# Turning the last pair's values one step later, and re-spacing the splits, row turns and early products of steps 46 to 63

## The chip, the cores and the metric

The kernel runs on one core of one Trainium2 chip. Its time is the device time of one execution in microseconds (us). Before the change the median of three runs is 1219.77 us (1219.66 to 1220.37).

The core has five engines that run side by side, each through its own list of instructions in order: TensorE (PE, matrix products and transposes), VectorE (DVE), ScalarE (ACT), GpSimd (POOL) and SyncE (SP), which here issues all DMA transfers. An instruction that needs another engine's result waits for it, and everything behind it on its own engine waits too.

## What is computed

One decoder layer on 1024 tokens of width 1024, in float32. Two mixers read one projection of the normalised input: an attention of eight heads with three dilated windows, and a gated linear recurrence (HGRN) of four heads. Their outputs, one beside the other, go through an output projection, then comes a feed-forward part.

```python
p = rmsnorm(x, mix_pre_norm) @ w_in            # q, k, v of attention; q, f, i, g of HGRN
A = dilated_mixture_attention(q_a, k_a, v_a)   # (window, dilation) = (128,1), (512,4), (2048,16)
R = hgrn2_recurrence(q_h, f_h, i_h, g_h)
x = x + rmsnorm(concat([rmsnorm(A), R]) @ w_out)
x = x + rmsnorm(square(relu(rmsnorm(x) @ w_ff1)) @ w_ff2)
```

## The kernel before

**Products.** Every float32 product is made of three matmuls (`three_pass`, L88 to L91): each factor is split into a high and a low part, and high by high, high by low and low by high are summed in PSUM. A split of a weight piece of 128x1024 is one instruction on ACT (L85, the high part) and one on DVE (L86, the low part); then SP issues the load of a later piece into a freed buffer (L106). `w_get(n, 0)` makes piece n available. The eight pieces of the output projection are WO0 to WO0+7: the first four belong to the HGRN half of its input, the last four to the attention half.

**PSUM.** There are four kinds of banks, two of each, used in turn: "mm" for projections, "s" for the attention's scores (looks), "t" for transposes (turns) and "pv" for weighted values. A bank is taken again once the engines that read it have done so.

**Attention.** The loop of 64 steps (8 heads of 8 items: D0 to D3 and F0, F1, N0, N1, the blocks of the dilated windows) is written out by hand, and the order of the code is the order on each engine. A step's parts are: `raise_` (ACT exponentials, L892), `look` (PE scores L837, L838, then DVE adds the bias table and takes the maximum, L842), `turn` (PE transposes the exponentials, L902, L911 or L914; ACT and DVE write high and low part, L924 to L932), `weigh` (PE multiplies with values, L948, L960, L966) and `finish` (PE transposes the result, L986, DVE sums, L990, POOL scales, L991). The bias table of a head comes from DRAM (`load_bias`, L798); that of the last head, number 7, goes into the tile `etable`.

**Filler.** Between these PE does units of other work, of three matmuls each: up to step 47 projections of later head pairs (`attn_proj`), from then on early products (`early_out`, tiles `pwe`), the HGRN half of the output projection for the first four row tiles, 32 units in all. `UNITS[head][item]` says how many units a step has; half of them, rounded down, stand ahead of the weigh, the rest behind it. An early product needs the row tile turned (`row_turn(t, 0)`, L1078, into `emt`) and the weight pieces; ACT moves its sum out (L1101, `esum`).

**Values of a pair.** The last step of a pair's projection multiplies its value half with a row factor on DVE (L764, tile `vf`, read from PSUM `pm_av`). `values_turn` (L712 to L726) transposes that on PE (L716, tile `pvt`), splits it (ACT L719, DVE L720), and for the second half SP writes the pair's values to DRAM (L723, four transfers `vd`). `far_load` (L642, six transfers, again called `vf`) then reads them back in another order for the far blocks F (L960). Pair 3 holds heads 6 and 7.

**Other pieces around the change.** `row_rec` (POOL, L1035) multiplies a row tile by a gain, `row_load` fetches a finished attention row, `row_norm` sums its squares on ACT (L1044, L1050), `row_gain` scales it on POOL. `hooks[s]` lists what step s does besides its fixed parts, after the first half of its units, the weigh and the finish. After step 63 come the late products (`late_out`, tiles `pwo`), the attention half of the output projection.

Of the kernel before, what the change touches and what calls it, by code (L numbers as in the profile page):

```python
# [25 lines left out]
AH = 8  # L26
# [11 lines left out]
def hymba_layer(ctx, tc, x, w_in, w_out, w_ff1, w_ff2, g_pre, lb_logits, g_mix, g_post,  # L38
# [17 lines left out]
    def bank(tag, name):  # L56
        return ps.tile([P, 512], F32, tag=tag, name=name,
                       bufs={"mm": 2, "s": 2, "t": 2, "pv": 2}[tag])
# [66 lines left out]
    def w_get(i, ahead=1):  # L125
        while done[1] < min(i + 1 + ahead, len(stream)):
            w_split()
        return parts[i]
# [26 lines left out]
    WO0 = len(stream)  # L155
# [13 lines left out]
    queue = []  # L169
# [17 lines left out]
    def drain():  # L187
        while queue:
            n = len(queue)
            fill(1e9)  # L190
            assert len(queue) < n or not queue
# [517 lines left out]
        for t in (kh, kl):  # L709
            nc.sync.dma_start(out=f32(t[c:d]), in_=f32(t[a:b]))  # L710

    def values_turn():  # L712
        pr, vs, full, hf = turn_later.pop(0)
        pt = bank("mm", f"pvt{pr}{hf}")
        for j in range(4):
            TE.transpose(pt[:, j * P:(j + 1) * P], full[:, j * P:(j + 1) * P], ident)  # L716
        ptv = pt.rearrange("p (j h d) -> p j h d", j=4, h=2)
        dst = vs[:, hf * 4:hf * 4 + 4]
        S.activation(dst[:, :, :, 0, :], ptv, AF.Copy)  # L719
        V.tensor_tensor(out=dst[:, :, :, 1, :], in0=ptv, in1=f32(dst[:, :, :, 0, :]), op=ALU.subtract)  # L720
        if hf == 1:
            for r in range(DIL):
                nc.sync.dma_start(out=v_dram[pr][r].rearrange("(n i) c -> i n c", i=32),  # L723
                                  in_=f32(vs[32 * r:32 * r + 32]).rearrange("p n h a d -> p n (h a d)"))
            if pr == 0:
                far_load(0)  # L726
# [68 lines left out]
    def load_bias(hd):  # L795
        if hd < AH and hd not in bts:
            bts[hd] = slab("BT", f"bt{hd}") if hd < AH - 1 else early["table"][:, 0]
            nc.sync.dma_start(out=bts[hd][:, :NEAR + FAR], in_=table_dram[hd])  # L798
# [201 lines left out]
    def load_gain(name, tag, src):  # L1000
        gains[name] = slab(tag, name)
        nc.sync.dma_start(out=gains[name], in_=src.partition_broadcast(P))

    NE = 4
# [14 lines left out]
    def early_sums():  # L1019
        early["sum"] = [wide.tile([P, 2, D], F32, tag="A", name=f"esum{q}") for q in range(NE // 2)]  # L1020
# [4 lines left out]
    def row_load(t):  # L1025
        row = rows[t] = slab("S", f"row{t}")
        c = AW if t < NE else 0
        nc.sync.dma_start(out=row[:, c:AW + AL], in_=mix_dram[t * P:(t + 1) * P, c:AW + AL])
# [4 lines left out]
    def row_rec(t):  # L1033
        gain = gains["early"] if t < NE else gains["gmix"][:, :AW]
        G.tensor_tensor(out=rec_row(t), in0=rec_row(t), in1=gain, op=ALU.mult)  # L1035
# [4 lines left out]
    def row_norm(t, which=(0, 1)):  # L1040
        row = rows[t]
        if 0 in which:
            ss = scales["part", t] = col("ass", 2)
            S.activation(half(f"dm{t}")[:, :AL], row[:, AW:AW + AL], AF.Square, accum_out=ss[:, 0:1])  # L1044
        if 1 not in which:
            return
        ss = scales.pop(("part", t))
        sa = col("asa")
        ra = scales["row", t] = tp.tile([P, 1], F32, tag="era", name=f"era{t}") if t < NE else col("ara")
        S.activation(half(f"dn{t}")[:, AL:AW], row_fin(t), AF.Square, accum_out=ss[:, 1:2])  # L1050
        G.tensor_tensor(out=sa, in0=ss[:, 0:1], in1=ss[:, 1:2], op=ALU.add)
        rsqrt_mean(ra, sa, AW, 1)
# [13 lines left out]
    def row_turn(t, which, late=False, tag="t"):  # L1066

        if t < NE and which == 0:
            dst = early["mt"][t // 2][:, t % 2]
        else:  # L1070
            if (t, 1) not in mts and (t, 0) not in mts or t < NE:
                mts[t] = slab("V8", f"mt{t}", F32R, (P, 2, 2, 4, P))
            dst = mts[t][:, which]
        mts[t, which] = dst
        src = rec_row(t) if which == 0 else rows[t][:, AW:]
        pt = bank("pv" if late else tag, f"pmt{t}_{which}")
        for j in range(4):
            TE.transpose(pt[:, j * P:(j + 1) * P], src[:, j * P:(j + 1) * P], ident)  # L1078
        split_into(dst[:, 0], dst[:, 1], pt.rearrange("p (j c) -> p j c", j=4))
# [12 lines left out]
    def early_out(t):  # L1092
        pms = [bank("mm", f"pwe{t}_{hf}") for hf in range(2)]
        for j in range(4):
            while j >= done[1] - WO0:
                yield None
            for hf, pm in enumerate(pms):
                sl = slice(hf * 512, hf * 512 + 512)
                three_pass(pm, [mts[t, 0][:, i, j] for i in range(2)], [w[:, sl] for w in parts[WO0 + j]], j == 0, j == 3)
                if j == 3:  # L1100
                    S.activation(early_sum(t)[:, sl], pm, AF.Copy)  # L1101
                yield 650.0
# [102 lines left out]
    for h in range(HH):  # L1205
# [5 lines left out]
        if not last:  # L1211
# [1 line left out]

    hooks = {
        0: lambda: last_gate(0),
        1: lambda: last_gate(1),
        43: lambda: row_rec(0),
        44: lambda: [row_rec(1), w_get(WO0, 0)],
        45: lambda: w_get(WO0 + 1, 0),
        46: lambda: [row_turn(0, 0), w_get(WO0 + 2, 0)],  # L1220
        47: lambda: [w_get(WO0 + 3, 0), row_rec(2)],
        49: lambda: [row_turn(1, 0), load_bias(AH - 1), row_rec(3)],
        51: lambda: row_turn(2, 0),
        52: lambda: load_gain("gmix", "R", g_mix),
        55: lambda: [row_load(t) for t in range(2)],
        57: lambda: [row_norm(t, (0,)) for t in range(2)],
        58: lambda: w_get(WO0 + 4, 0),
        59: lambda: [row_norm(0, (1,)), row_gain(0), row_load(2)],
        60: lambda: [row_norm(1, (1,)), row_gain(1)],
        61: lambda: row_turn(0, 1, tag="t"),  # L1230
        62: lambda: w_get(WO0 + 5, 0),
        63: lambda: w_get(WO0 + 6, 0),
    }
    UNITS = ((2, 3, 3, 4, 3, 3, 3, 3), (2, 3, 3, 4, 3, 3, 3, 3), (3, 3, 3, 4, 2, 3, 3, 2), (3, 3, 3, 4, 2, 3, 3, 2),
             (3, 3, 3, 3, 2, 3, 3, 2), (3, 3, 3, 3, 2, 2, 2, 2), (3, 2, 2, 3, 2, 2, 2, 1), (2, 2, 2, 3, 1, 2, 2, 1))
    ITEMS = (("D", 0), ("D", 1), ("D", 2), ("D", 3), ("F", 0), ("F", 1), ("N", 0), ("N", 1))
    LOOKS = {0: ((0, "D", 2), (0, "N", 1)), 1: ((0, "D", 3), (0, "F", 0)), 2: ((0, "F", 1),),
             6: ((1, "D", 0),), 7: ((1, "D", 1),)}
# [3 lines left out]
    for s in range(n_steps):  # L1242
        hd, i = divmod(s, 8)
        if s % 16 == 3:
            first_done[s // 16] = True
        elif s % 16 == 11:
            second_done[s // 16] = True
        ready, to_weigh = to_weigh, []
        if i in (3, 4):
            joint(hd, int(i == 4))  # L1250
        coming = (hd, *ITEMS[i + 1]) if i < 7 else (hd + 1, *ITEMS[0])
        raise_(*coming, which=(0,))
        if s % 16 in (11, 13) and s < n_steps - 16:
            while keys_done[s // 16 + 1] < (1 if s % 16 == 11 else 2):
                fill(1.0)
        looks = LOOKS.get(i, ())
        for d, kind, g in looks[:1]:
            look(hd + d, kind, g)
        kind, g = ITEMS[i]
        turn(hd, kind, g)  # L1260
        raise_(*coming, which=(1,))
        if i == 0:
            far_queries(hd)
        if kind != "D" or g % 2:
            to_weigh.append((hd, kind, g // 2 if kind == "D" else g))
        units = UNITS[hd][i]
        for _ in range(units // 2):
            fill(0.0, True)
        to_fold, last_fold = [(*w, r) for w in ready for r in [weigh(*w)] if r is not None], to_fold
        for d, kind, g in looks[1:]:  # L1270
            look(hd + d, kind, g)
        for *w, r in last_fold:
            finish(*w, *r)
        if i in (0, 2):
            spread_max(hd, int(i == 2))
        elif i == 5:
            send(hd)
        elif i == 6:
            receive(hd)
        if i in (1, 2, 3, 6, 7):  # L1280
            key_job()
        if s == 47:
            drain()
            values_turn()
            early_sums()
            queue.extend(early_out(t) for t in range(NE))
        if s % 16 == 15 and s < n_steps - 1:
            far_load(s // 16 + 1)
        hooks.get(s, lambda: None)()
        for _ in range(units - units // 2):  # L1290
            fill(0.0, True)
        if i in (1, 3):
            swap_max(hd, int(i == 3))
        if i == 7:
            look(hd + 1, "N", 0)
        if s == 53:
            row_turn(3, 0, tag="s")
    for *w, r in to_fold:
        finish(*w, *r)
    drain()  # L1300
# [904 lines left out]
```

## Time and profile before

| | |
|---|---|
| median of three runs | 1219.77 us |
| the profiled execution | 1219.76 us |
| its span, first to last instruction | 1218.0 us |
| PE busy | 1200.7 us, 99% of the span |
| DVE, ACT, POOL busy | 71%, 45%, 27% |
| steps 46 to 63 in the trace | about 462 to 524 us |
| mean granted clock of PE over the span | 0.997 |

In rows of waits the engine and line that waited stand first, then the engine and line that ended the wait, then us in total, times, and the longest. In a timeline a row has start, duration, engine, line, operation, out<-in and shape; a number in brackets at its end is the idle time before it and what ended it. PE matmuls are pipelined: the distance between two starts is what one costs, and its duration is longer. The granted clock is the share of full speed that PE was given.

### The profile page before, as it was taken

Reading aid. Unit: us, or ns where it says so; the run is one execution under the profiler, and the core shown is the slowest. Engines: PE = TensorE matmul, PEld = TensorE weight load, DVE = VectorE, ACT = ScalarE, POOL = GpSimd, SP = SyncE. Lnnn points to the kernel's source line nnn. Section 1 sums busy time; section 2 is a strip of 40 time slices with the busy share of each in tenths; the row PEclk is TensorE's granted clock in tenths of the full one; section 3 lists DMA queues with packets and bytes.
Section 4 is the critical chain, followed back from the end, with each engine's and each line's share of the span. In section 5 each row is a group of like instructions: output and inputs, shape, how many; then the busy total and the mean of one; then the engine's idle time right before and its main releaser. Section 6 shows DMA issues by size and latency. Waiting matters only on the chain.

```text
span 1218.0 us, 17222 instructions
## 1 busy us (share of the span) xinstructions
PE 1200.7 (99%) x6350; PEld 1028.1 (84%) x6350; DVE 868.3 (71%) x1478; ACT 546.9 (45%) x1067; POOL 323.4 (27%) x321
## 2 busy tenths in 40 slices
PE   8999999999999998999999999999999999999998
PEld 8898989888888887878888888888888888888886
DVE  5697878776766767668589567666678454488796
ACT  7633333322665667755565132222234453534562
POOL 0110102022221223245240876665722000000022
PEclk9999999999999999999999999999999999999999
DMA  5221323123443646264425446454587534433337
GB/s 217 68 94 57 113 66 97 47 81 83 133 120 104 156 109 166 77 208 136 172 77 174 172 157 228 178 185 152 190 316 267 216 100 156 156 104 94 115 104 276
DMA packets 86483, 174.21 MB, mean 143 GB/s; under 512 B 12160, under 2 KB 38784, under 8 KB 86400
## 3 DMA queue, kind: packets, MB, share of 16 engines
q1 hardware_dynamic: 86400, 173.12, 43.7%
q8 instruction: 50, 0.82, 0.3%
q14 instruction: 33, 0.27, 0.1%
HBM read 117.76 MB, written 49.04 MB: 137 GB/s over the span
## 4 chain that ended last, share of the span: by engine, by line
PE 94%; ACT 2%; DVE 2%; issue 1%; DMA 1%; SPq 0%; POOL 0%; DVEq 0%; POOLq 0%; ACTq 0%
PE f L1945 18%; PE f2s L1945 7%; PE pig L91 2%; PE pig L89 2%; PE pig L90 2%; PE pl L480 2%; PE pwo L90 2%; PE pwo L91 2%; PE pwo L89 2%; PE pm_f L89 1%; PE pm_ak L89 1%; PE pm_f L91 1%; PE pm_f L90 1%; PE pm_ak L91 1%; PE pm_ak L90 1%; PE pm_av L89 1%
## 5 line engine op out<-in xcount | busy, mean ns | idle before, releaser
L86 DVE TENSOR_TENSOR al<-ar,ah 128x1024 fp32r<-128x1024 f32 x56 | 70.6, 1260 | 80.2 <-ACT ah L85 77.7
L1945 PE MATMUL f<-bh,al 128*128 128x512 f32 x320 | 124.5, 389 | 0.0
L1945 PE MATMUL f<-bh,ah 128*128 128x512 f32 x320 | 124.5, 389 | 0.0
L1945 PE MATMUL f<-bl,ah 128*128 128x512 f32 x320 | 124.5, 389 | 0.0
L85 ACT ACTIVATE ah<-ar 128x1024 fp32r<-128x1024 f32 x56 | 59.1, 1056 | 86.2 <-DMA ar<-actd 85.9
L1945 PEld LDWEIGHTS f<-bh,al 128*128 128x128 f32 x320 | 60.1, 188 | 12.6
L1945 PEld LDWEIGHTS f<-bl,ah 128*128 128x128 f32 x320 | 60.1, 188 | 12.5
L1945 PEld LDWEIGHTS f<-bh,ah 128*128 128x128 f32 x320 | 60.1, 188 | 12.3
L2019 POOL TENSOR_SCALAR lbl<-ssq 128x1 f32<-128x1 f32 x4 | 3.3, 818 | 245.5 <-ACT fd L2015 245.4
L1568 POOL TENSOR_TENSOR e<-x,e 128x512 f32<-128x512 f32 x14 | 21.6, 1540 | 131.3 <-DVE x L1519 131.3
L1945 PE MATMUL f2s<-bh,al 128*128 128x512 f32 (+1 forms) x128 | 49.0, 382 | 0.0
L1945 PE MATMUL f2s<-bl,ah 128*128 128x512 f32 (+1 forms) x128 | 48.9, 382 | 0.0
L1945 PE MATMUL f2s<-bh,ah 128*128 128x512 f32 (+1 forms) x128 | 48.9, 382 | 0.0
L671 POOL COPY tout<-traw 128x256 f32<-128x256 f32 x16 | 12.4, 775 | 109.7 <-DMA traw<-in_bias_tab_dram 76.1
L991 POOL TENSOR_TENSOR anat<-anat,stat 128x128 f32<-128x128 f32 (+1 forms) x24 | 12.4, 515 | 108.2 <-DVE anat L990 91.2
L86 DVE TENSOR_TENSOR bl<-br,bh 128x1024 fp32r<-128x1024 f32 x32 | 40.1, 1252 | 1.2 <-ACT bh L85 1.1
L1962 ACT ACTIVATE acc<-f 128x512 f32<-128x512 f32 x28 | 16.8, 598 | 50.0 <-PE f L1945 50.0
L86 DVE TENSOR_TENSOR wl<-raw,wh 128x1024 fp32r<-128x1024 f32 x23 | 30.6, 1331 | 11.0 <-ACT wh L85 11.0
L85 ACT ACTIVATE bh<-br 128x1024 fp32r<-128x1024 f32 x32 | 33.6, 1051 | 4.2 <-PE f L1945 3.1
L707 POOL TENSOR_TENSOR kl<-kf,kh 64x512 fp32r<-64x512 f32 x16 | 22.2, 1389 | 39.2 <-ACT kh L706 37.1
L751 POOL TENSOR_TENSOR ql<-qf,q 64x512 fp32r<-64x512 f32 x16 | 21.4, 1336 | 42.3 <-ACT q L750 41.7
L89 PE MATMUL pwo<-woh,mt 128*128 128x512 f32 x80 | 31.8, 398 | 0.4 <-ACT woh L85 0.4
(1702 smaller groups left out, 4023.7 us busy)
## 6 DMA issues: line engine op xcount, KB each, us to landing
ar<-actd SPq DMA_DIRECT2D x56, 512.0 KB, 3.7
br<-in_w_ff_dram SPq DMA_DIRECT2D x16, 1024.0 KB, 5.9
w1r<-in_w_ff_dram SPq DMA_DIRECT2D x14, 1024.0 KB, 6.5
raw<-in_w_in_dram SPq DMA_DIRECT2D x26, 512.0 KB, 3.7
actd<-e SPq DMA_DIRECT2D x17, 768.0 KB, 4.3
actd<-e SPq DMA_DIRECT2D x11, 1024.0 KB, 4.1
vd<-v SPq DMA_DIRECT2D x16, 256.0 KB, 4.1
raw<-in_w_out_dram SPq DMA_DIRECT2D x8, 512.0 KB, 3.7
```

The lines of the kernel that those rows point to most:

```text
L85: S.activation(hi, src, AF.Copy)
L86: eng.tensor_tensor(out=lo, in0=src, in1=f32(hi), op=ALU.subtract)
L89: TE.matmul(dst, lhs[0], rhs[0], start=start, stop=False)
L90: TE.matmul(dst, lhs[0], rhs[1], start=False, stop=False)
L91: TE.matmul(dst, lhs[1], rhs[0], start=False, stop=stop)
L480: TE.matmul(pl[:, n % 2, :192], kt[:, n * P:(n + 1) * P], sets[u // 2][:, n % 4], start=True, stop=True)
L671: G.tensor_copy(by_class(dst[:, part_ * w:(part_ + 1) * w]), in_blocks(raw[:, FAR * DIL:]))
L707: G.tensor_tensor(out=kl[a:b], in0=src, in1=f32(kh[a:b]), op=ALU.subtract)
L751: G.tensor_tensor(out=lo[a:b], in0=full[a:b], in1=f32(stacks[i]["q"][a:b, sl]), op=ALU.subtract)
L1568: eng[0].tensor_tensor(out=e1[:, 3], in0=a21, in1=e1[:, 2], op=ALU.add)
L1945: TE.matmul(pm, a[:, j, c], b[:, j, d], start=start and j == 0 and q == 0, stop=stop and j == 1 and q == 2, skip_group_check=True)
L1962: S.activation(acc_at(p, i), pm, AF.Copy)
```

## The change

The second half of pair 3's values is turned in step 48, behind that step's looks and in a bank "t", where it was turned in step 47 in a bank "mm"; its far load goes with it. In step 47 the rest of the projection is drained first, and then WO0+2 is split, so that split stands behind the read of the projection on DVE. WO0+3 is split in step 48, behind the values. WO0+4 goes from step 58 to 55 and WO0+5 from 62 to 61. Four row turns, two row loads, a row product on POOL and a row norm move by one to three steps, and the gate of the last HGRN head from step 1 to 2. Of the units, one of a projection goes from step 46 to step 35; steps 47, 48, 51 and 52 have one less each, and steps 60 and 63 one more; the early products stay 32 in all.

```diff
-    def values_turn():
+    def values_turn(tag="mm"):
         pr, vs, full, hf = turn_later.pop(0)
-        pt = bank("mm", f"pvt{pr}{hf}")
+        pt = bank(tag, f"pvt{pr}{hf}")
...
     hooks = {
         0: lambda: last_gate(0),
-        1: lambda: last_gate(1),
+        2: lambda: last_gate(1),
         43: lambda: row_rec(0),
         44: lambda: [row_rec(1), w_get(WO0, 0)],
         45: lambda: w_get(WO0 + 1, 0),
-        46: lambda: [row_turn(0, 0), w_get(WO0 + 2, 0)],
-        47: lambda: [w_get(WO0 + 3, 0), row_rec(2)],
-        49: lambda: [row_turn(1, 0), load_bias(AH - 1), row_rec(3)],
-        51: lambda: row_turn(2, 0),
-        52: lambda: load_gain("gmix", "R", g_mix),
-        55: lambda: [row_load(t) for t in range(2)],
-        57: lambda: [row_norm(t, (0,)) for t in range(2)],
-        58: lambda: w_get(WO0 + 4, 0),
+        46: lambda: row_turn(0, 0),
+        47: lambda: [drain(), w_get(WO0 + 2, 0), early_sums(), queue.extend(early_out(t) for t in range(NE))],
+        48: lambda: [values_turn("t"), far_load(AH // 2 - 1), w_get(WO0 + 3, 0), row_rec(2)],
+        49: lambda: [load_bias(AH - 1), row_rec(3)],
+        50: lambda: row_turn(1, 0),
+        52: lambda: [row_turn(2, 0), load_gain("gmix", "R", g_mix)],
+        54: lambda: row_turn(3, 0),
+        55: lambda: [w_get(WO0 + 4, 0), row_load(0)],
+        57: lambda: [row_load(1), row_norm(0, (0,))],
+        58: lambda: row_norm(1, (0,)),
         59: lambda: [row_norm(0, (1,)), row_gain(0), row_load(2)],
         60: lambda: [row_norm(1, (1,)), row_gain(1)],
-        61: lambda: row_turn(0, 1, tag="t"),
-        62: lambda: w_get(WO0 + 5, 0),
+        61: lambda: w_get(WO0 + 5, 0),
+        62: lambda: row_turn(0, 1),
         63: lambda: w_get(WO0 + 6, 0),
     }
...
-             (3, 3, 3, 3, 2, 3, 3, 2), (3, 3, 3, 3, 2, 2, 2, 2), (3, 2, 2, 3, 2, 2, 2, 1), (2, 2, 2, 3, 1, 2, 2, 1))
+             (3, 3, 3, 4, 2, 3, 3, 2), (3, 3, 3, 3, 2, 2, 1, 1), (2, 2, 2, 2, 1, 2, 2, 1), (2, 2, 2, 3, 2, 2, 2, 2))
...
-        if s == 47:
-            drain()
-            values_turn()
-            early_sums()
-            queue.extend(early_out(t) for t in range(NE))
-        if s % 16 == 15 and s < n_steps - 1:
+        if s in (15, 31):
             far_load(s // 16 + 1)
...
-        if s == 53:
-            row_turn(3, 0, tag="s")
```

On DVE in step 47 there stood, before (ptNl is the low part of a turned N block, emt that of the turned row tile, wol that of WO0+2, vf the last read of the projection, v the low part of the turned values):

```order
L932 TENSOR_TENSOR ptNl_5003<-pt_N_5001,ptNh_5002 128x4x128
L86 TENSOR_TENSOR emt_4794<-pmt_0_5025,emt_4794 128x512
L86 TENSOR_TENSOR wol_5033<-raw_4951,woh_5032 128x1024
L764 TENSOR_TENSOR vf_5041<-pm_av_4908,rrow 128x512
L842 ISA pf_4995,stat_4993<-ps_D_5044,bt_4680 128x256
L842 ISA stat_4993 128x1
L845 TENSOR_SCALAR stat_4993<-stat_4993 128x1
L932 TENSOR_TENSOR ptNl_5003<-pt_N_5049,ptNh_5002 128x4x128
L720 TENSOR_TENSOR v_4568<-pvt_5060,v_4568 128x8x64
```

and now, at the same place:

```order
L932 TENSOR_TENSOR ptNl_5006<-pt_N_5004,ptNh_5005 128x4x128
L86 TENSOR_TENSOR emt_4778<-pmt_0_5025,emt_4778 128x512
L764 TENSOR_TENSOR vf_5035<-pm_av_4899,rrow 128x512
L842 ISA pf_4998,stat_4996<-ps_D_5038,bt_4683 128x256
L842 ISA stat_4996 128x1
L845 TENSOR_SCALAR stat_4996<-stat_4996 128x1
L932 TENSOR_TENSOR ptNl_5006<-pt_N_5043,ptNh_5005 128x4x128
L86 TENSOR_TENSOR wol_5055<-raw_4954,woh_5054 128x1024
L842 ISA pn_5067,stat_4996<-ps_N_5068,bt_4683 128x256
```

The split wol went from ahead of vf to behind the second ptNl, where the reads of step 48's scores (pn) stand behind it; v left this stretch.

On PE the transposes pvt stood behind step 47's weigh (pov_far) and ahead of the first early unit (pwe):

```order
L966 MATMUL pov_far<-ptNh_5002,v_3907 128x4x64
L966 MATMUL pov_far<-ptNl_5003,v_3907 128x4x64
L716 MATMUL pvt_5060<-ident,vf_5041 128x128 x4
L89 MATMUL pwe_0_5088<-wh_4947,emt_4794 128x512
L90 MATMUL pwe_0_5088<-wl_4948,emt_4794 128x512
L91 MATMUL pwe_0_5088<-wh_4947,emt_4794 128x512
L837 MATMUL ps_N_5094<-kh_0_4671,q_0_4431 128x256
L838 MATMUL ps_N_5094<-kl_0_4672,q_0_4431 128x256
```

and now they stand in step 48, behind the looks ps_N of its end:

```order
L837 MATMUL ps_N_5099<-kh_0_4671,q_0_4431 128x256
L838 MATMUL ps_N_5099<-kl_0_4672,q_0_4431 128x256
L716 MATMUL pvt_5108<-ident,vf_5035 128x128 x4
L89 MATMUL pwe_0_5062<-woh_4986,emt_4778 128x512
L90 MATMUL pwe_0_5062<-wol_4987,emt_4778 128x512
L91 MATMUL pwe_0_5062<-woh_4986,emt_4778 128x512
L837 MATMUL ps_D_5138<-kh_0_4671,q_0_4431 128x512
L838 MATMUL ps_D_5138<-kl_0_4672,q_0_4431 128x512
L902 MATMUL pt_D_5143<-ident,pf_4998 128x128 x2
```

So pvt moved behind two units, three looks, a turn and a weigh.

On ACT in steps 58 to 60 the split woh of WO0+4 stood between two evictions of early products (esum) and ahead of the exponentials pf, with dn, a row's sum of squares, behind them:

```order
L1101 ACTIVATE esum_5072<-pwe_0_5356 128x512
L951 ACTIVATE pf_5329<-pov_0_5490 128x256
L85 ACTIVATE woh_5498<-raw_5036 128x1024
L1101 ACTIVATE esum_5072<-pwe_1_5357 128x512
L892 ACTIVATE pf_5329,stat_5327<-pf_5329,stat_5327 128x192
L931 ACTIVATE pth_2_5479<-pt_D_5511 128x4x128
L892 ACTIVATE pf_5329,stat_5327<-pf_5329,stat_5327 128x192
L1050 ACTIVATE dn_5531,ass<-anat_5234 128x128
```

and now:

```order
L951 ACTIVATE pf_5312<-pov_0_5483 128x256
L1044 ACTIVATE dm_5492,ass<-row_5454 128x384
L892 ACTIVATE pf_5312,stat_5310<-pf_5312,stat_5310 128x192
L931 ACTIVATE pth_2_5473<-pt_D_5500 128x4x128
L892 ACTIVATE pf_5312,stat_5310<-pf_5312,stat_5310 128x192
L1050 ACTIVATE dn_5518,ass<-anat_5229 128x128
L1101 ACTIVATE esum_5061<-pwe_0_5419 128x512
L1101 ACTIVATE esum_5061<-pwe_1_5420 128x512
```

The split is gone from here, and the evictions of the third row tile's early products stand behind dn.

## The prediction

> **What bounds the kernel now.** I read the page first (busy shares), then PE's waits in the stretch that the change touches, then the granted clock there, and last the queues of PE, DVE, SP and ACT around the largest wait.
>
> ```profile
> span 1218.0 us, 17222 instructions
> PE 1200.7 (99%) x6350; PEld 1028.1 (84%) x6350; DVE 868.3 (71%) x1478; ACT 546.9 (45%) x1067; POOL 323.4 (27%) x321
> ```
>
> PE is the bound; only the time in which it stands still, or runs at a lower clock, can be won. Its waits between 460 and 540 us (total, times, longest):
>
> ```profile
> PE pvt L716 <- DVE vf L764: 3.0, 1, 3.0
> PE pt_F L914 <- ACT pf L892: 1.5, 2, 1.0
> PE pwo L90 <- DVE wol L86: 0.8, 1, 0.8
> PE pt_N L911 <- DVE ptNl L932: 0.7, 1, 0.7
> PE pov_far L966 <- ACT ptNh L931: 0.6, 1, 0.6
> PE pov_far L966 <- DVE ptNl L932: 0.5, 1, 0.5
> PE pwo L89 <- ACT woh L85: 0.4, 1, 0.4
> ```
>
> They are 7.5 us in eight waits, in steps 47, 60, 61 and 63 and the first late product. The windows of that stretch and of the work behind it (sum, PE, PEld, DVE, ACT, POOL, granted clock, DMA share, GB/s):
>
> ```profile
> 470.00:471.00 1.00, 0.53 (x3) 0.54 (x4) 0.96 (x5) 0.00 (x0) 0.00 (x0) 0.50 1.09 215
> 512.00:514.00 2.00, 1.05 (x6) 0.64 (x6) 1.00 (x3) 1.94 (x11) 1.87 (x4) 1.00 0.01 2
> 528.00:560.00 32.00, 32.00 (x158) 26.66 (x158) 26.23 (x37) 16.64 (x52) 22.26 (x40) 1.00 0.67 224
> ```
>
> So the clock is at half right behind the 3.0 us wait, and not in 512 to 514, where PE works 1.05 of 2.00 us. From 528 us on PE doesn't wait: what is won or lost before it moves the end by as much. PE's timeline, step 47 to 48 and the same places in steps 55 and 56:
>
> ```profile
> 467.14 0.28 PE L966 MATMUL pov_far<-ptNl,v 128*128 128x256 f32 x1
> 470.47 1.11 PE L716 MATMUL pvt<-ident,vf 128*128 128x128 f32 x4 [3.04 <-DVE vf L764]
> 471.23 0.78 PE L89 MATMUL pwe<-wh,emt 128*128 128x512 f32 x1
> 473.80 0.48 PE L89 MATMUL pwe<-wh,emt 128*128 128x512 f32 x1
> 495.20 0.28 PE L838 MATMUL ps_D<-kl,q 128*128 128x256 f32 x1
> 495.32 0.60 PE L911 MATMUL pt_N<-ident,pn 128*128 128x128 f32 x4
> 495.68 0.31 PE L966 MATMUL pov_far<-ptNh,v 128*128 128x128 f32 x1
> 496.22 0.40 PE L89 MATMUL pwe<-wh,emt 128*128 128x512 f32 x1
> 496.92 0.28 PE L837 MATMUL ps_N<-kh,q 128*128 128x256 f32 x1
> 497.78 0.48 PE L89 MATMUL pwe<-woh,emt 128*128 128x512 f32 x1
> ```
>
> Three prices come from it. The slow clock: from 471.23 to 473.80 PE does in 2.57 what takes 1.56 in step 56 (496.22 to 497.78), and the four transposes ahead take 0.76 against 0.36 (495.32 to 495.68), so 1.4 us. The tail: a matmul of 0.28 is followed after 0.12 when nothing waits (495.20, 495.32), so each wait costs some 0.16 beyond its listed length. A unit (three matmuls): 0.70 (496.22 to 496.92).
>
> **What goes.** DVE around the 3.0 us wait, POOL beside it, and SP and its landings behind it:
>
> ```profile
> 464.04 1.22 DVE L86 TENSOR_TENSOR wol<-raw,woh 128x1024 fp32r<-128x1024 f32 x1
> 465.57 0.68 DVE L932 TENSOR_TENSOR ptNl<-pt_N,ptNh 128x512 fp32r<-128x512 f32 x1
> 467.35 2.11 DVE L86 TENSOR_TENSOR wol<-raw,woh 128x1024 fp32r<-128x1024 f32 x1 [0.39 <-ACT woh L85]
> 469.38 1.03 DVE L764 TENSOR_TENSOR vf<-pm_av,rrow 128x512 f32<-128x512 f32 x1
> 471.62 0.60 ACT L719 ACTIVATE v<-pvt 128x512 fp32r<-128x512 f32 x1 [3.44 <-PE pvt L716]
> 472.25 0.69 DVE L720 TENSOR_TENSOR v<-pvt,v 128x512 fp32r<-128x512 f32 x1 [0.71 <-ACT v L719]
> 467.11 1.27 POOL L1035 TENSOR_TENSOR erows<-erows,etable 128x512 f32<-128x512 f32 x1
> ```
> ```profile
> 472.97 3.06 SPq L723 DMA_DIRECT2D vd<-v  x4
> 478.60 3.91 SPq L642 DMA_DIRECT2D vf<-vd  x6
> 483.66 0.86 SPq L798 DMA_DIRECT2D etable<-tabd  x1
> gmix<-in_g_mix_dram SPq DMA_DIRECT2D x1, 512.0 KB, 7.3
> etable<-tabd SPq DMA_DIRECT2D x1, 352.0 KB, 6.8
> 490.40 0.22 PE L960 MATMUL pov_far<-ptFh,vf 128*128 128x128 f32 x1
> 493.88 0.28 DVE L842 CUSTOM_DVE_ANT_0 pd<-ps_D,etable 128x128 f32<-128x128 f32 x1
> ```
>
> Before, the eviction vf (L764) stands behind a split of WO0+2 of 2.11 us that itself waits 0.39 for ACT; PE stands at the transposes pvt until it is done. After, vf follows emt directly, and pvt comes behind the looks of step 48, some 5 us of PE work later. The 3.0 and the 1.4 go. Behind it in steps 59 to 61 stands another split, with what it delays on ACT:
>
> ```profile
> 507.09 1.22 DVE L86 TENSOR_TENSOR wol<-raw,woh 128x1024 fp32r<-128x1024 f32 x1 [1.10 <-ACT woh L85]
> 508.62 0.46 ACT L892 ACTIVATE pf<-pf,stat 128x192 f32<-128x192 f32 x1 [1.08 <-DVE stat L879]
> 511.28 0.31 ACT L1050 ACTIVATE dn<-anat 128x128 f32<-128x128 f32 x1 [1.19 <-POOL anat L991]
> ```
>
> It (WO0+4) moves from step 58 to 55, and step 60 gets a second unit as cover: the two pt_F waits (1.5) go. Step 63 gets units between the two weighs where none was left: both pov_far waits (1.1) go. The last splits come a step earlier: the pwo waits (1.2) go but for a rest. pt_N (0.7) stays, and is priced anew below. The eight tails are 1.3. So 7.5 + 1.3 + 1.4 = 10.2 us go.
>
> **What comes.** The matmuls are the same 6350: the unit added in step 35 is the one missing in 46, and the early units missing in 48 to 58 follow by 63. I let PE's new order run with the distances of the rows above, and each engine's new order with its own durations, from step 46, where PE is 0.7 later than before; tails included:
> - pt_N of step 47 needs the bank that ptNl (465.57) frees. DVE ends that 0.7 us later, PE arrives at the same time, having one unit less. 0.7 + 0.7 + tail, on about 1.6; bounds 0.9 (DVE not later) and 2.4.
> - ps_N of step 48 needs a bank read by DVE behind the moved split of WO0+2. That now runs behind ptNl, without POOL's L1035 beside it, so at 1.22 (464.04), not 2.11. PE waits 0.9; bounds 0 and 1.8 (with 2.11).
> - ps_F of step 50: DVE's v split now stands behind pvt of step 48 (PE ends it at about 473.1; ACT 0.6, DVE 0.69: 474.4), the split of WO0+3 behind that (475.9), and two reads of the next look behind it (477.8). PE is there at 476.7: 1.15; bounds 0 and 2.0.
> - pt_F of steps 52 and 53: the same shape as steps 60 and 61 before (0.6 and 0.95 with one unit of cover), but without a split ahead of ACT's pf. 0.35; bounds 0 and 1.85 (that pattern whole, with tails).
> - SP: v is whole at 474.4 against 472.94 (472.25 + 0.69), so vd, vf and the table of head 7 are issued 1.5 later: vf at 480.1 to 484.0, etable at 485.2, landed after 6.8 at 492.0. PE is by then ahead of before: pov_far of step 53 comes at 487.0, not 490.40, and vf has landed by 487. DVE would read the table (493.88 before) at 489.5; it stands until 492.0, ptNl stands behind it, and pt_N of step 55 goes at 493.0 where PE came at 492.0. 1.0; bounds 0 (table 1 us sooner) and 1.5 (the 7.3 of gmix).
> - Steps 56 to 63 and the first late product: small waits behind the split now in 55, an eviction that now stands behind ACT's dn (511.28) in step 60, and the last weight piece. 0.9; bounds 0 and 2.4 (half of what these places lose before: 3.8 and six tails, 4.8).
>
> Sum 5.9. A rest of the moves costs nothing. The row turns are the same four transposes of 0.36 in other gaps, and row loads are asked for two steps after they are issued. The gate of the last HGRN head goes from step 1 to 2:
>
> ```profile
> 312.39 1.12 DVE L610 SCALAR_TENSOR_TENSOR gate<-po,hrs,gate 128x128 f32<-128x128 f32 x4
> ```
>
> PE has no wait for what follows it there or in step 2, and DVE has idle time behind it in both; bounds 0 and 1.1, I take 0. The extra unit of step 35 pulls a weight split ahead of ACT's pf for step 36; the wait of that kind in step 60 was 0.6, so 0 to 0.75, and I take 0, for PE's transposes there come a unit later as well.
>
> Net 10.2 - 5.9 = 4.3 us. The profiled execution took 1219.76 (span 1218.0 and 1.76 around it), the median of the three runs is 1219.77, so one stands for the other: 1219.8 - 4.3 = 1215.5.
>
> On the port that DVE and POOL share: the rows have 2.11 us for a split beside POOL's L1035 and 1.22 without it. The Trainium skill (SBUF — State Buffer, "Who interferes with whom") says that a VectorE instruction with two SBUF inputs contends with a GpSimd instruction that reads SBUF. The trace agrees, and by this rule the vf eviction, with one input in PSUM, may stand beside L1035 as it now does; were it wrong, vf's 1.03 would be longer and the sum up to 0.9 smaller.
>
> **The rivals.**
> - The waits only move. If the terms of steps 47 to 53 reach their upper bounds (ptNl 0.8, the slow split 0.9, ps_F 0.85, pt_F 1.5 more: 4.05), the gain is eaten: 1219.5. For it: DVE's chain has the same work, and PE gets less cover in steps 48 to 53, where early units are taken out. Against: POOL is clear of the split, and no split is left behind pf. 0.15.
> - SP's chain decides, the slower side. v, vd, vf, table are one row of waits; each us that the table lands later than 492.0 costs PE one. At 496.3, 11 us after issue, nothing is won, and at 498.7 the kernel is 2.4 us (0.2%) slower: 1222.2. For it: the chain starts 1.5 later while PE is ahead, and its old margin is spent. Against: the slowest row near, gmix, took 7.3. 0.11.
> - The clock falls again behind a new wait. The waits of step 47 (1.6) or step 50 lie between the 3.0 after which it was at 0.50 and the 512:514 window, in which half the time was idle and it stayed at 1.00. Price 1.4: 1216.9. 0.08. The Trainium skill (TensorE: Matmul & The Clock Gate, "Part 1: The HAM clock gate") gives a free-running window of about 3.4 us: half rate after an idle one, full after a busy one. By it nothing falls here, as by my sum; but here a wait of 3.04 was enough, so the trace has it lower than a whole window.
> - Less comes than I priced. The table lands 1 us sooner and ps_F finds its bank free: 1213.4. 0.10.
>
> **How the numbers follow.** The forecast has 0.56, alone 1214 to 1217.2. What a measurement of this kernel can tell is about 0.2%, 2.4 us: faster is below 1217.4, slower above 1222.2. Faster: 0.56 + 0.10 + half the clock's 0.08 = 0.70. Same: 0.15 + 0.04 = 0.19. Slower: 0.11. The bounds of the new terms add up to 0.9 and 12; the joint range that I give leaves out the half of the fourth rival below 1213 and SP's upper part, and reaches past the "waits only move" case: 1213.0 to 1220.2.
>
> **What would show it.** Right: no wait of pvt, a granted clock of 1.00 from 460 to 540, DVE waiting for DMA at its first read of etable, and pt_N of step 55 behind it; waits at pt_N (47), ps_N (48) and ps_F (50) of 0.7 to 1.6; none at pt_F in 60 and 61, none at pov_far of 63. Wrong: a wait at pov_far of step 53 for vf's DMA, one over 2 us at ps_N or ps_F, or PE waiting after 528 us.

## The result and the profile after

The changed kernel takes 1214.18 us (median of five runs, 1213.34 to 1214.51), the kernel before 1219.66 beside it: a ratio of 0.9954, interval 0.994 to 0.9969. It is 5.5 us faster, where 4.3 were forecast. The profiled execution took 1214.51, with a span of 1212.7 us.

Three marks on PE show where the 5.3 us of span lie: the first product, an instruction px well ahead of the changed steps, and the second row turn of the late products. Before, and after:

```profile
8.96 0.36 PE L89 MATMUL pig<-wig0h,hTh 128*128 128x256 f32 x1
396.32 0.28 PE L873 MATMUL px<-pick,swap 128*128 128x4 f32 x2
533.04 0.60 PE L1078 MATMUL pmt<-ident,row 128*128 128x128 f32 x4
```
```profile
8.70 0.37 PE L89 MATMUL pig<-wig0h,hTh 128*128 128x256 f32 x1
396.05 0.28 PE L873 MATMUL px<-pick,swap 128*128 128x4 f32 x2
528.01 0.60 PE L1078 MATMUL pmt<-ident,row 128*128 128x128 f32 x4
```

From the first mark to the second it is 387.36 and 387.35 us: the gate's move in steps 1 and 2 cost nothing. From the second to the third, the stretch in what follows, it is 136.72 and 131.96: 4.76 are won there. From the third to the end it is 684.96 and 684.69. The remaining 0.26 is the first product's own start, which differs by up to 1.2 us between the profiles of this study (7.78 to 8.96) and has nothing to do with the change. So a run's verdict rests on its median, and its mechanism on its stretch, which is that of one execution. Two executions, the profiled one of the run with POOL splits and an earlier table (1706.84 us) and one of the run with four idle products (4274.34), were disturbed and are left out below.

PE's waits from 460 to 540 us after the change (total, times, longest):

```profile
PE pt_N L911 <- DVE ptNl L932: 0.9, 2, 0.7
PE ps_F L837 <- DVE stat L842: 0.7, 1, 0.7
PE pov_far L960 <- DMA vf<-vd: 0.7, 1, 0.7
PE ps_N L837 <- DVE stat L842: 0.5, 1, 0.5
PE pwe L89 <- ACT esum L1101: 0.5, 1, 0.5
PE ps_D L837 <- DVE stat L842: 0.4, 1, 0.4
PE pt_F L914 <- DVE ptFh L929: 0.3, 1, 0.3
PE pt_F L914 <- ACT pf L892: 0.2, 1, 0.2
```

The waits at pvt, at pov_far for ACT and DVE and at pwo are gone, those at pt_F of steps 60 and 61 too (the two rows of pt_F are now steps 52 and 53), and the clock is at 1.00 where it was at half; PE still doesn't wait behind the stretch (sum, PE, PEld, DVE, ACT, POOL, clock, DMA share, GB/s):

```profile
470.00:472.00 2.00, 1.46 (x13) 1.32 (x12) 1.97 (x10) 1.19 (x2) 0.00 (x0) 1.00 0.39 54
525.00:555.00 30.00, 30.00 (x149) 25.06 (x149) 25.20 (x35) 15.79 (x50) 20.30 (x37) 1.00 0.69 227
```

DVE, POOL and SP, from the values' read to the table:

```profile
460.77 1.23 DVE L86 TENSOR_TENSOR wl<-raw,wh 128x1024 fp32r<-128x1024 f32 x1 [0.86 <-ACT wh L85]
467.03 1.08 DVE L764 TENSOR_TENSOR vf<-pm_av,rrow 128x512 f32<-128x512 f32 x1
469.16 1.21 DVE L86 TENSOR_TENSOR wol<-raw,woh 128x1024 fp32r<-128x1024 f32 x1
472.97 0.69 DVE L720 TENSOR_TENSOR v<-pvt,v 128x512 fp32r<-128x512 f32 x1
491.65 0.29 DVE L842 CUSTOM_DVE_ANT_0 pd<-ps_D,etable 128x128 f32<-128x128 f32 x1 [2.70 <-PE pmt L1078]
459.57 3.57 POOL L1035 TENSOR_TENSOR erows<-erows,etable 128x512 f32<-128x512 f32 x2
467.27 1.30 POOL L1035 TENSOR_TENSOR erows<-erows,etable 128x512 f32<-128x512 f32 x1
```
```profile
473.69 3.04 SPq L723 DMA_DIRECT2D vd<-v  x4
479.44 3.64 SPq L642 DMA_DIRECT2D vf<-vd  x6
484.24 0.58 SPq L798 DMA_DIRECT2D etable<-tabd  x1
etable<-tabd SPq DMA_DIRECT2D x1, 352.0 KB, 7.2
```

The read vf stands no longer behind a split (467.03, before 469.38). The values are whole 0.7 us later than before (473.66, before 472.94; 1.0 when counted from the second mark), and with them the row on SP; the table lands at 491.4 (484.24 + 7.2), and DVE, which had been idle for 2.7, goes on at 491.65.

Two details of the change as it was run: of the row loads only that of row 1 moves, from step 55 to 57, and the turn of row tile 3 takes a bank "t", where it took a bank "s".

### The profile page after: what moved, and what is told of

It is laid out like the page before. It is cut to its first block, busy times and chain, and to the rows that moved or that the text cites. A ratio compares the mean times of both kernels' runs of the same rounds, so it can differ in the third digit from the quotient of the medians.

```text
span 1212.7 us, 17220 instructions
## 1 busy us (share of the span) xinstructions
PE 1198.3 (99%) x6350; PEld 1026.8 (85%) x6350; DVE 868.8 (72%) x1478; ACT 546.6 (45%) x1067; POOL 326.3 (27%) x321
## 4 chain that ended last, share of the span: by engine, by line
PE 93%; DVE 2%; ACT 2%; DMA 1%; issue 1%; POOL 0%; SPq 0%; DVEq 0%; POOLq 0%; ACTq 0%
PE f L1940 18%; PE f2s L1940 7%; PE pig L91 2%; PE pig L89 2%; PE pig L90 2%; PE pl L480 2%; PE pwo L91 2%; PE pwo L89 2%; PE pwo L90 2%; PE pm_ak L89 1%; PE pm_f L89 1%; PE pm_ak L91 1%; PE pm_ak L90 1%; PE pm_f L91 1%; PE pm_f L90 1%; PE pm_av L89 1%
```

## The experiments

**The two halves apart.** One run moves the values' turn and the splits of WO0+2 and WO0+3 alone, the other makes the rest of the change alone.

```diff
-        46: lambda: [row_turn(0, 0), w_get(WO0 + 2, 0)],
-        47: lambda: [w_get(WO0 + 3, 0), row_rec(2)],
+        46: lambda: row_turn(0, 0),
+        47: lambda: [drain(), w_get(WO0 + 2, 0), early_sums(), queue.extend(early_out(t) for t in range(NE))],
+        48: lambda: [values_turn("t"), far_load(AH // 2 - 1), w_get(WO0 + 3, 0), row_rec(2)],
```

> Before, with the values' turn in step 48 (bank t), the split of WO0+2 behind the projection's read and that of WO0+3 behind the values; the units, row turns and later splits stay as before. My theory (the time is PE's waits with 0.16 us of tail each, and the slow clock): the wait at pvt (3.2 with tail) and the slow clock (1.4) go, waits at ps_D and ps_N of step 48 come (0.5 and 0.7), ps_F of step 50 is covered by the units left in 48, the waits of steps 60 to 63 and of the late product (4.8 with tails) stay: 1216.3, granted clock 1.00 in steps 47 and 48. Rival, the re-spacing of the units is what brings the gain: near 1219.

Measured: 1216.04 us, ratio 0.9971 (0.996 to 0.9981); the stretch is 132.92, 3.80 shorter. The second run is the changed kernel with these lines the other way round:

> The changed kernel with the values' turn and the splits of WO0+2 and WO0+3 put back into steps 46 and 47. My theory: the waits of steps 60 to 63 and of the late product (4.8) go but for 0.7, pt_F of 52 and 53 costs 0.8, pvt's wait and the slow clock stay: 1216.4. With the first run the two halves would win 3.4 and 3.3, together more than the 5.5 of the whole change, because the waits for the far load (0.9) and the table (0.4) come only when both are made. Rival, the halves add up to the whole: 1217.5 and 1216.3 or the like, and the far load's wait stands in one of them.

Measured: 1216.51, ratio 0.9974 (0.9964 to 0.9984); the stretch is 133.58, 3.14 shorter. Both came out as my theory had them, and the rivals fall: neither half is the whole. The halves add up to 6.9 against the 4.76 of the whole. The 2.2 are the waits that only the whole change has: ps_D of step 48 (0.52 with tail), ps_F (0.90), vf (0.90) and pt_N of step 55 (0.41), 2.7, less the 0.6 by which pvt waits longer in the second run (3.66, before 3.04):

```profile
470.85 0.66 PE L716 MATMUL pvt<-ident,vf 128*128 128x128 f32 x4 [3.66 <-DVE vf L764]
```

The slow clock behind that wait should take some 0.3 more there, an estimate from the last section, so about 0.4 of the 2.2 stays open. In the first run ps_D and ps_F did not wait. I put that down to the units left in steps 47 and 48, which no run tests alone; I had forecast 0.5 for ps_D.

**Only the split's place.**

```diff
-        46: lambda: [row_turn(0, 0), w_get(WO0 + 2, 0)],
-        47: lambda: [w_get(WO0 + 3, 0), row_rec(2)],
+        46: lambda: row_turn(0, 0),
+        47: lambda: [w_get(WO0 + 2, 0), w_get(WO0 + 3, 0), row_rec(2)],
```

> Before, with only the split of WO0+2 moved behind the values' turn in step 47 (the values are still turned in 47). My theory: pvt waits 0.6 instead of 3.0 and the clock does not fall, but the two splits of WO0+2 and WO0+3 then stand one behind the other on DVE ahead of the reads of step 48's looks, and ps_N waits about 1.4: 1217.4. Rival, the split's place is all there is to it and the turn's place does nothing: the same as the first run, 1216.3 or less.

Measured: 1218.25, ratio 0.9989 (0.998 to 0.9998); the stretch is 134.92, 1.80 shorter. In the profile:

```profile
467.52 0.66 PE L716 MATMUL pvt<-ident,vf 128*128 128x128 f32 x4 [0.56 <-DVE vf L764]
472.89 0.39 PE L837 MATMUL ps_N<-kh,q 128*128 128x256 f32 x1 [1.69 <-DVE stat L842]
```

The cause of the 3.0 us wait is the split ahead of vf: behind it, pvt waits 0.56. But two splits in one place make the looks wait 1.69, so the move of this split alone does not bring what the first run brought, and the rival falls. What the run does not separate: in the change WO0+3 also gets a step to itself. Whether that would do with the values still turned in step 47, where pvt would keep its 0.56, was not run. The time is 0.85 over my figure and its eleven runs lie 3.3 us apart (1216.60 to 1219.86); the four with a mean clock of 0.999 lie from 1216.6 to 1218.1, the seven with 0.997 or 0.998 from 1217.0 to 1219.9. I infer that the clock falls in some executions of this kernel and not in others; the profiled one has it at 1.00.

**The table ahead of the far load.**

```diff
-        47: lambda: [drain(), w_get(WO0 + 2, 0), ...
-        49: lambda: [load_bias(AH - 1), row_rec(3)],
+        47: lambda: [load_bias(AH - 1), drain(), w_get(WO0 + 2, 0), ...
+        49: lambda: row_rec(3),
```

> The changed kernel with head 7's table asked for in step 47, ahead of vd and vf on SP. My theory: DVE's idle time of 2.7 at its first read of etable goes, and with it the wait of pt_N in step 55 (0.25, 0.41 with tail); the wait for vf in step 53 (0.74) stays: 1213.8. Rival, the order on SP is the lever and the far load then suffers by the table's 0.6 to 0.9 ahead of it: 1214.5 or more, with a longer wait for vf.

Measured: 1213.55, ratio 0.9951 (0.9938 to 0.9963); the stretch is 130.58, 1.4 shorter than the changed kernel's. By the medians it is 0.6, which the two intervals do not tell apart. The rows:

```profile
468.08 0.59 SPq L798 DMA_DIRECT2D etable<-tabd  x1
etable<-tabd SPq DMA_DIRECT2D x1, 352.0 KB, 4.6
488.79 0.29 DVE L842 CUSTOM_DVE_ANT_0 pd<-ps_D,etable 128x128 f32<-128x128 f32 x1
```

DVE's read of the table comes at 488.79 without idle time: the 2.7 us in the changed kernel were the table's, though the profile there puts them down to a row turn that ended in the same instant. The wait of pt_N in step 55 goes, as forecast. The far load does not suffer; its wait of 0.74 is gone too, which I had not forecast. Its slowest transfer landed after 4.4 us here and after 5.3 in the changed kernel. That the table, issued behind it there, slowed it is not shown, and one run speaks against it: the run with the split of WO0+4 put back (below) has the table behind the far load as well, its slowest transfer landed after 4.2, and nothing waited for it. There the table itself cost 1.01 at pt_N. So what its place is worth lies between 0.41 (the changed kernel's profile) and 1.17 (that run's), with tails; that the 0.90 at vf is gone here may be luck.

**DVE's chain eased.** The low parts of WO0+2 and WO0+3 are made on POOL: `w_split(G)` splits the next piece with POOL in DVE's place.

```diff
-        47: lambda: [drain(), w_get(WO0 + 2, 0), ...
-        48: lambda: [values_turn("t"), far_load(AH // 2 - 1), w_get(WO0 + 3, 0), row_rec(2)],
+        47: lambda: [drain(), w_split(G), ...
+        48: lambda: [values_turn("t"), far_load(AH // 2 - 1), w_split(G), row_rec(2)],
```

> The changed kernel with the low parts of WO0+2 and WO0+3 made on POOL instead of DVE. My theory (DVE's chain sets the waits of steps 48 to 50): the waits at ps_N (0.7 with tail) and ps_F (0.9) go, that at ps_D (0.5) stays, the values are split some 0.5 us earlier and the wait for vf (0.9) shrinks by as much: 1212.0. Rival: POOL takes 2.5 us for each (1.27 for half the size), the early products wait for them, and the gain is lost: 1214 or more.

Measured: 1214.08, ratio 0.9952 (0.994 to 0.9964): no gain by the median over the changed kernel's 1214.18, where I expected 2.2; the stretch, 131.24, is 0.7 shorter. The waits at ps_N and ps_F are gone, so DVE's chain did cause them, and POOL's 2.40 us for each split delayed nothing. But the waits reappear further on:

```profile
486.00 0.30 PE L960 MATMUL pov_far<-ptFh,vf 128*128 128x128 f32 x1 [1.03 <-DMA vf<-vd]
490.44 0.29 DVE L842 CUSTOM_DVE_ANT_0 pd<-ps_D,etable 128x128 f32<-128x128 f32 x1 [3.44 <-DMA etable<-tabd]
491.58 0.66 PE L911 MATMUL pt_N<-ident,pn 128*128 128x128 f32 x4 [1.02 <-DVE ptNl L932]
```

Counted from the second mark, the far load starts 0.4 us sooner than in the changed kernel and PE comes more than 1 us sooner: 0.74 and 0.25 became 1.03 and 1.02. With the table's load moved as well:

> The run before with head 7's table also asked for in step 47. My theory: 1211.6, no wait left at pt_N of step 55. Rival, the chain on SP is not what is late once DVE is free: the same time as with the POOL splits alone, within 0.3 us.

Measured: a ratio of 0.9952 (0.994 to 0.9963), five runs from 1211.97 to 1216.25, and no row to say what waited. By the ratio it is the run before again, as the rival had it. But the runs are too far apart to tell 0.3 us, and in the pair that follows the same move gained 1.3, so I take this one as undecided.

**The values sooner.** With the POOL splits, the values are turned at the end of step 47, where PE stands waiting for ps_D.

```diff
         if i == 7:
             look(hd + 1, "N", 0)
+        if s == 47:
+            values_turn("t")
+            far_load(AH // 2 - 1)
```

> The kernel with the POOL splits, with the values turned at the end of step 47, behind its look, where PE waits 0.5 us for ps_D in any case; head 7's table stays where it was. My theory now: with DVE's chain eased, the row v, vd, vf, table on SP is what PE waits for (1.2 at pov_far of 53 and 1.2 at pt_N of 55, with tails); v comes some 2 us sooner, so both waits and ps_D's go: 2.5 us less than with the POOL splits alone, about 1211.5. Rival, the waits of 53 and 55 come from the load on the DMA engines there and not from the start of the row: they stay near 1 us each and the time is that of the POOL splits, 1214.

Measured: 1212.83, ratio 0.9943 (0.9931 to 0.9956); the stretch is 130.72, 0.5 shorter than with the POOL splits alone.

```profile
471.61 3.50 SPq L723 DMA_DIRECT2D vd<-v  x4
478.48 3.66 SPq L642 DMA_DIRECT2D vf<-vd  x6
485.96 0.30 PE L960 MATMUL pov_far<-ptFh,vf 128*128 128x128 f32 x1 [0.32 <-DMA vf<-vd]
491.79 0.66 PE L911 MATMUL pt_N<-ident,pn 128*128 128x128 f32 x4 [1.25 <-DVE ptNl L932]
```

Half of my theory held: ps_D's wait is gone and vf's is 0.32, not 1.03. But an earlier start is not handed on in full. From the first vd to the first vf it is 6.9 us here, 5.75 in the changed kernel (473.69 to 479.44), and from the second mark the table landed 0.5 us sooner than in the run with the POOL splits alone, while PE came to it 0.7 sooner: pt_N of step 55 waits 1.25. With the table in step 47 too:

> The same with the table asked for in step 47 too. My theory: the row on SP is early enough without it, so no more than 0.4 us (pt_N of 55) below the run before. Rival, the table's place is the larger lever: 1 us or more below.

Measured: 1211.55, ratio 0.9932 (0.992 to 0.9944). That is 1.3 below the run before, so the rival held. By the stretch (129.43) the table's place is the larger lever, 1.3 against 0.5; by the medians the two moves gained alike, 1.3 each. This kernel, 8.4 us below the kernel before beside it (1219.91), has the lowest median of the study. Left in its stretch are pt_N of step 47 (0.7), vf (0.5), pwe (0.5) and two small pt_F (0.3 and 0.2).

**The split of WO0+4 put back.**

```diff
-        55: lambda: [w_get(WO0 + 4, 0), row_load(0)],
-        58: lambda: row_norm(1, (0,)),
+        55: lambda: row_load(0),
+        58: lambda: [row_norm(1, (0,)), w_get(WO0 + 4, 0)],
```

> The changed kernel with the split of WO0+4 put back from step 55 to 58, the second unit of step 60 kept. My theory: the split stands ahead of stat and pf again, and pt_F of step 60 waits about 1.3 (PE comes to it sooner than before), that of 61 less than before: 1215.6. Rival, the second unit of step 60 was what took the two waits away: 1214.2.

Measured: 1218.24, ratio 0.9989 (0.998 to 0.9998); the profiled execution took 1215.80, with these waits:

```profile
506.28 0.33 PE L914 MATMUL pt_F<-ident,pf 128*128 128x128 f32 x1 [0.51 <-ACT pf L892]
507.20 0.44 PE L914 MATMUL pt_F<-ident,pf 128*128 128x128 f32 x2 [0.59 <-ACT pf L892]
509.27 0.50 PE L89 MATMUL pwe<-wh,emt 128*128 128x512 f32 x1 [1.64 <-ACT esum L1101]
```

The 1.1 us of pt_F answer the 1.3 I had; the wait of pwe, 0.5 in the changed kernel, grew by 1.1 beside it, because dn and esum stand behind the same late pf on ACT. The rival falls: the split's place took these waits away; to the second unit at most the 0.4 is left by which they are shorter than before (1.5). The median is 2.4 above the profiled execution, and most runs have a mean clock of 0.996 to 0.998 where that one had 0.999: I infer that three waits close together let the clock fall in most executions.

Up to step 55 this kernel is the changed one, and there its profile has something to add. The two waits behind SP's row, in the changed kernel and then here:

```profile
487.95 0.30 PE L960 MATMUL pov_far<-ptFh,vf 128*128 128x128 f32 x1 [0.74 <-DMA vf<-vd]
492.79 0.66 PE L911 MATMUL pt_N<-ident,pn 128*128 128x128 f32 x4 [0.25 <-DVE ptNl L932]
```
```profile
490.70 0.29 DVE L842 CUSTOM_DVE_ANT_0 pd<-ps_D,etable 128x128 f32<-128x128 f32 x1 [2.97 <-DMA etable<-tabd]
491.84 0.66 PE L911 MATMUL pt_N<-ident,pn 128*128 128x128 f32 x4 [1.01 <-DVE ptNl L932]
```

With the same instructions, and vd and vf issued at the same distance from the second mark within 0.1 us, here PE did not wait for vf and waited 1.01 at pt_N, as the prediction had it. Which of the two waits shows is a matter of the execution; their sum, with tails, is 1.31 and 1.17.

**The price of the clock.** Idle products on DVE, two in one run and four in another, lengthen the wait of pt_N in step 47.

```diff
-        45: lambda: w_get(WO0 + 1, 0),
+        45: lambda: [w_get(WO0 + 1, 0), pad(2)],
...
+    def pad(count):
+        z = half("pad")
+        for _ in range(count):
+            V.tensor_tensor(out=z, in0=rrow[:, :512], in1=rrow[:, 512:], op=ALU.mult)
```

> The changed kernel with two idle products of 128x512 on DVE ahead of ptNl in step 46 (they feed nothing). PE's wait at pt_N of step 47 grows from 0.67 by their length, about 0.65 each, to 2.0. My theory: the time grows by 1.3 and no more, 1215.5, for the clock does not fall after 2.0. Rival, it falls after 2 us already: 1216.9.

Measured: 1215.96, ratio 0.9966 (0.9953 to 0.9978). The wait and the windows behind it:

```profile
466.93 0.66 PE L911 MATMUL pt_N<-ident,pn 128*128 128x128 f32 x4 [2.22 <-DVE ptNl L932]
466.00:468.00 2.00, 1.07 (x8) 1.07 (x9) 1.97 (x6) 0.87 (x3) 1.92 (x2) 0.88 0.61 166
468.00:470.00 2.00, 2.00 (x8) 1.71 (x8) 1.97 (x6) 1.73 (x4) 0.37 (x1) 0.50 0.91 173
470.00:472.00 2.00, 2.00 (x11) 1.79 (x11) 1.97 (x8) 0.73 (x2) 0.00 (x0) 0.77 0.07 14
```

My theory that the clock stays up after 2 us falls. It fell, half a microsecond after PE had gone on. The stretch is 132.62, 0.66 longer than the changed kernel's: 1.55 of wait, less 2.53 of waits that are gone because PE comes later (ps_D, ps_N, vf, pt_N of step 55, with tails), plus 1.6, which is left for the clock. The times alone would not have told: the execution at the median, 1215.96, has a mean clock of 1.000, the profiled one, 1214.76, has 0.998.

> The same with four idle products: the wait at pt_N grows to about 3.3, as long as that of pvt before. My theory, the clock's fall costs 1.4 beside the wait: 2.6 + 1.4, 1218.2, mean granted clock 0.997. Rival, the slow clock was hidden behind DVE (PE would have waited anyway): 1216.8, whatever the clock does. A second rival, a wait below the window of 3.4 us that the Trainium skill gives (TensorE: Matmul & The Clock Gate, Part 1: The HAM clock gate) leaves the clock alone: 1216.8 with a mean clock of 0.999.

Measured: 1219.81, ratio 0.9999 (0.9991 to 1.0008), mean clock 0.996. The four idle products took longer than planned, and so the wait was 5.55:

```profile
464.16 4.95 DVE L1217 TENSOR_TENSOR pad<-rrow 128x512 f32<-128x512 f32 x4
470.16 1.12 PE L911 MATMUL pt_N<-ident,pn 128*128 128x128 f32 x4 [5.55 <-DVE ptNl L932]
```

The stretch is 137.70, 5.74 longer than the changed kernel's: 4.88 of wait, less 1.22 (ps_D and ps_N gone), plus 0.14 at vf and pt_N, and 1.9 for the clock, which is at half for PE's first 4.6 us of work. So the slow clock costs time of its own, and the rival that it was hidden falls. For the second rival this wait was too long to be a test; the run with two products, whose clock fell after 2.22 us, speaks against it.

## Why the prediction was right

It was right in sign and mechanism, and 1.2 us short in size. By its own terms, in us with tails:

| term | forecast | measured |
|---|---|---|
| waits, tails and clock that go | 10.2 | all gone at their places |
| pt_N, step 47 | 1.6 | 0.83 |
| ps_D, step 48 | not seen | 0.52 |
| ps_N, step 48 | 0.9 | 0.70 |
| ps_F, step 50 | 1.15 | 0.90 |
| pt_F, steps 52, 53 | 0.35 | 0.79 |
| vf, step 53 | 0 | 0.90 |
| table, pt_N of step 55 | 1.0 | 0.41 |
| steps 56 to 63 | 0.9 | 0.66 (pwe) |
| sum that comes | 5.9 | 5.71 |

10.2 - 5.7 = 4.5, against 4.76 in the stretch; 0.27 more came behind it, which no term had, and 0.26 of the profiled execution is the start.

That the sum of what comes was met so closely (5.9, 5.71) is luck in part. The misses of its terms add up to 3.9 without their signs and cancel to 0.2 with them. And of the three signs that the prediction names against itself one was seen: PE waited at pov_far of step 53 for vf's DMA. The signs that it names for itself were all seen, but ps_N, with 0.54, waited less than the 0.7 named.

- *What goes.* Shown by the two halves: pvt's wait goes with the values' half, those of pt_F, pov_far and pwo with the other. That it was the split ahead of vf is shown by its move alone, that it was the split ahead of pf by putting it back. That a slow clock costs time of its own is shown by the idle products (1.6 and 1.9); the 1.4 here is by the rows alone.
- *pt_N of step 47.* I had DVE 0.7 later; it wasn't. Before, the split in front (wl) took longer, beside the same two products of POOL:

```profile
460.62 1.84 DVE L86 TENSOR_TENSOR wl<-raw,wh 128x1024 fp32r<-128x1024 f32 x1 [0.87 <-ACT wh L85]
458.83 2.54 POOL L1035 TENSOR_TENSOR erows<-erows,etable 128x512 f32<-128x512 f32 x2
```

  After, it is DVE 1.23 and POOL 3.57: the loss passed from DVE to POOL, which nobody waits for. The Trainium skill (SBUF — State Buffer, "Who interferes with whom") has this as a matter of which instruction comes first, not of its shape. The rows agree, by an estimate: one product of POOL took 1.27 (467.11, before), so the second of the two would start at 460.10 before, ahead of the split (460.62), and at 460.84 after, behind it (460.77). The vf read, with one input in SBUF, took 1.08 beside L1035 (467.27), against 1.03 alone, so it may stand there, as the prediction had it by that section's rule.
- *ps_D of step 48* was missed: I let DVE's emt end in time, but it waited 0.6 for ACT, and ps_D for the read behind it.
- *SP's row.* Its place and its price were right, the order of its two waits was not: one of the six vf transfers took 5.3 us, not 4.3, so PE waited in step 53, and that wait hid most of the table's. Forecast 1.0 for the two, measured 1.31. In the run with the split of WO0+4 put back the order was the forecast one (0 and 1.17, with tail), so the step that failed is that vf has landed when PE comes to it: it had in one execution and not in the other.
- *The rivals.* The waits did not merely move, since the split runs at 1.21 without POOL's L1035, and none is left ahead of pf. SP's row was not 4.3 later than priced but 0.3 sooner: the table landed at 491.4, 491.7 with the 0.27 by which the second mark lies earlier, against 492.0. The clock did not fall in the profiled execution. But it was nearer than I thought: I had weighed waits of 1.6 against the 3.0 that made it fall, and 2.2 was enough in the run with two idle products.

## What to carry over

A wait on the bounding engine is best traced to the instruction that stands in front on the other engine's list; moving that one instruction took the largest wait here, but it needed a free place elsewhere, and the same move without it won 1.4 us, not 5.5. Once an engine's chain is eased, ask which transfer PE now reaches too soon: here most of the gain on DVE was taken back at two loads until they were issued earlier, and the table, which needs nothing of the chain ahead of it, was the cheap one to move. Where two waits hang on one row of transfers, forecast their sum; which of them shows can change from one execution to the next. Price a long wait with the clock that may fall behind it; several short ones close together may do the same, which is inferred here.

## What the hardware showed that I had not expected

In the profiles of this study the clock, once it falls, is slow for a fixed time or twice that. Finer windows show its fall and rise before the change, in the second half alone and with the idle products: 469.88 to 473.29, 471.47 to 474.88, 467.51 to 470.92 (two products) and 467.96 to 474.79 (four). For example, before, where a mean clock of 0.70 in a window of 0.20 means full speed for the first 0.08:

```profile
469.80:470.00 0.20, 0.00 (x0) 0.00 (x0) 0.20 (x1) 0.00 (x0) 0.00 (x0) 0.70 1.18 328
...
473.20:473.40 0.20, 0.20 (x3) 0.20 (x3) 0.20 (x1) 0.20 (x1) 0.00 (x0) 0.77 0.00 0
```

That is 3.41 us three times, and 6.83 once. The Trainium skill (TensorE: Matmul & The Clock Gate, "Part 1: The HAM clock gate") gives a free-running window of 3.4 us; the lengths agree. But it speaks of an idle window as what lowers the clock, and here the 3.4 us ahead of the fall were idle for 2.2 (two products), 2.5 (before) and 2.8 (second half alone) only. So by these rows the price is half of the time that PE works while the clock is slow, up to 1.7 us for 3.41. That makes 1.4 before, 1.7 with two products and 2.3 with four, where the sums above have 1.4, 1.6 and 1.9: the last is 0.4 off, and why stays open. Near 2 us of idle time the place of the window may decide, which would explain why the clock falls in some executions of one kernel and not in others; that is inferred, since only one profile of each was seen.
